# Halved weight sums and a two-step S4 in the paired projections of a fused two-block kernel

## The chip, the cores and the metric

The kernel runs on 1 core of one Trainium2 chip. The metric is the device time of one execution in microseconds (us). Five engines work side by side, each through its own queue in order: TensorE (PE, with its weight loads shown as PEld), VectorE (DVE), ScalarE (ACT), GpSimd (POOL) and SyncE (SP), which here only issues transfers.

## The reference, cut to what matters

Two transformer blocks follow each other on 1024 tokens of width 1024, in float32. The change touches two of the projections in them:

```
# pool layer of block 1
u, z = split(h @ w_in, [1024])              # w_in: 1024 x 2048
p    = multiscale_pool(u)                   # windowed means minus u
y    = ((einsum(p, w_mix) * scale) * silu(z)) @ w_out
# feed-forward of block 2
h    = h + square(relu(m @ w_up)) @ w_down  # w_up: 1024 x 4096
```

In both cases it is the first product (`h @ w_in` and `m @ w_up`) that is concerned.

## The kernel before, in words

Each float32 operand is written as a high and a low part (hi + lo), and each product takes three matmuls, hi by hi, lo by hi and hi by lo (`mm3`, L104, lines L108, L110 and L111). The high part is a copy on ScalarE, the low part the operand less the high part; `split_evac` (L117) does both, with the subtraction on VectorE unless another engine is named.

`project_pairs` (L327) computes a projection with a Winograd-type scheme of seven half-size products instead of eight. The activations, transposed, lie as quadrants A11, A12, A22 and the sums S1 to S4; the weights of a pair of column blocks (128 columns each, raw tiles r1 and r2) are turned into sums by `weight_sums` (L358, four subtractions on VectorE): the top half of r2, both halves of a third tile tt, and the bottom half of r1. `split_group` (L272) then splits such a raw tile of 128 x 1024 into `whi` (cast on ScalarE, L275) and `wlo` (subtraction on GpSimd, L276).

It is called twice: for the pool layer (L992, 8 pairs, NF=5) and for the feed-forward (L1952, 16 pairs, NF=4). Each call has two stretches.

- **The opening.** NF pairs do their first two products (`first_two`, A11 and A12), while the loop over j = 0 to 3 (L417) transposes the second half of the rows on TensorE (`turned`, L282), and `sums(j)` (L385) makes S2, A21 (for S1), A22, S3 and S4 of slice j, each with its hi and lo part. S4 = A12 - S2 is the last of them (L407), followed by its split (L408). A12 itself comes from the argument `a12`. In the feed-forward it lies there as a full float32 tile. In the pool layer it doesn't: GpSimd adds the high and the low part into a stage tile (L413), and L407 reads that. Between j = 1 and j = 2 the first pair's weights are summed (L435), and after j = 2 its tt tile is split (L437, `g0`).
- **The pairs.** `pair(p, ...)` (L443) sums and splits the weights and does S2, S1, S3, S4 and A22, of which S2 and S3 read the top half (LO) of a split tile and S1 and S4 the bottom half (HI). tt is split at L452, r2 at L457 and the bottom half of r1 at L467. All matmuls of one product go to one PSUM bank; there are 8 banks, and the bank of S2 and S3 is read by VectorE (`res.add`) before A22 may write it.

In the pool layer `Pooled` (L864) does the windowed sums of the finished u blocks on VectorE between the pairs (`doubled`, `less_u`, `cut`), with two tiny GpSimd products each (L949, L950), and zeroes the head of each u tile on GpSimd (L881). `stage()` (L846) there hands out eight half tiles in turn, cut from two u tiles, a z tile and a sum tile; the same pools hold the u and z blocks of the pairs.

The queues of the engines don't stand in the order of the source: a scheduler sets them when the program is built, by when it expects each instruction's inputs, and `issue_after` holds single instructions behind others. Buffers whi, wlo and wraw have three tiles each.

## Time and profile before

| what | value |
|---|---|
| median of 3 runs | 2354.05 us (2352.31 to 2356.96) |
| the profiled execution | 2356.74 us |
| its span, first to last instruction | 2354.9 us |
| mean granted TensorE clock | 0.990 of full |
| busy: PE / DVE / ACT / POOL | 2281.8 / 1504.1 / 1020.2 / 785.5 us |

The profile is of one execution. An engine's busy share is its time in instructions against the span. The pool layer's projection runs from about 450 to 640 us in the span, that of the feed-forward from about 1720 to 2025 us. A timeline row gives start, duration, engine, line, operation, output and inputs, and in square brackets the idle time before it with what ended it. A name is that of the first tile of a group, so the stage tiles appear as u, z and sum, and the line of a helper stands for all that call it.

### The profile page before, as it was taken

Reading aid. Unit: us, or ns where it says so; the run is one execution under the profiler, and the core shown is the slowest. Engines: PE = TensorE matmul, PEld = TensorE weight load, DVE = VectorE, ACT = ScalarE, POOL = GpSimd, SP = SyncE. Lnnn points to the kernel's source line nnn. Section 1 sums busy time; section 2 is a strip of 40 time slices with the busy share of each in tenths; the row PEclk is TensorE's granted clock in tenths of the full one; section 3 lists DMA queues with packets and bytes.
Section 4 is the critical chain, followed back from the end, with each engine's and each line's share of the span. In section 5 each row is a group of like instructions: output and inputs, shape, how many; then the busy total and the mean of one; then the engine's idle time right before and its main releaser. Section 6 shows DMA issues by size and latency. Waiting matters only on the chain.

```text
span 2354.9 us, 32237 instructions
## 1 busy us (share of the span) xinstructions
PE 2281.8 (97%) x11910; PEld 1900.3 (81%) x11910; DVE 1504.1 (64%) x2724; ACT 1020.2 (43%) x1921; POOL 785.5 (33%) x535
## 2 busy tenths in 40 slices
PE   7999999989998999999999999999999999999997
PEld 6877777867877888878988888888778888878886
DVE  5566676688788355554165746668785444687775
ACT  5344452543355354553232322423575555533334
POOL 2112123345532344431222112114324444454455
PEclk9999999999999999999999999999999999999999
DMA  4111013433372222211111111358145444754231
GB/s 159 39 28 37 19 36 108 134 85 108 111 256 94 63 59 68 54 59 46 46 47 52 50 54 44 122 181 312 65 136 197 149 150 171 279 209 171 101 125 72
DMA packets 248942, 253.10 MB, mean 107 GB/s; under 512 B 61064, under 2 KB 183006, under 8 KB 244944
## 3 DMA queue, kind: packets, MB, share of 16 engines
q1 hardware_dynamic: 239968, 233.38, 30.5%
q10 hardware_dynamic: 8224, 16.00, 1.8%
q0 software_dynamic: 592, 1.65, 0.3%
q8 instruction: 94, 1.54, 0.3%
q14 instruction: 64, 0.52, 0.1%
HBM read 181.26 MB, written 69.46 MB: 106 GB/s over the span
## 4 chain that ended last, share of the span: by engine, by line
PE 60%; DVE 11%; issue 3%; DMA 2%; ACT 2%; POOL 1%; SPq 0%; DVEq 0%; ACTq 0%; POOLq 0%
PE mm L110 18%; PE mm L108 18%; PE mm L111 18%; PE A L1550 2%; PE PT L1314 1%; DVE xl L119 1%; PE S L1291 1%; DVE sum L226 1%; PE tp L1570 1%; DVE raw L226 1%; DVE s L1303 1%; DVE xh L119 0%; DMA st<-d_y 0%; ACT ea L1050 0%; PE mm L282 0%
## 5 line engine op out<-in xcount | busy, mean ns | idle before, releaser
L108 PE MATMUL mm<-xh,whi 128*128 128x512 f32 (+2 forms) x1616 | 624.6, 387 | 11.6 <-DVE z L226 4.7
L110 PE MATMUL mm<-xl,whi 128*128 128x512 f32 (+2 forms) x1616 | 617.7, 382 | 0.0
L111 PE MATMUL mm<-xh,wlo 128*128 128x512 f32 (+2 forms) x1616 | 614.3, 380 | 0.2 <-POOL wlo L80 0.2
L80 POOL TENSOR_TENSOR wlo<-wraw,whi 128x1024 fp32r<-128x1024 f32 (+1 forms) x99 | 233.7, 2364 | 738.1 <-ACT whi L79 673.7
L108 PEld LDWEIGHTS mm<-xh,whi 128*128 128x128 f32 x1616 | 307.4, 190 | 70.1 <-DVE z L226 5.6
L111 PEld LDWEIGHTS mm<-xh,wlo 128*128 128x128 f32 x1616 | 307.1, 190 | 58.5 <-POOL wlo L80 0.5
L110 PEld LDWEIGHTS mm<-xl,whi 128*128 128x128 f32 x1616 | 307.5, 190 | 50.8
L111 PE MATMUL mm<-whi,xl 128*128 128x512 f32 (+1 forms) x752 | 272.0, 362 | 0.0
L79 ACT CAST whi<-wraw 128x1024 fp32r<-128x1024 f32 (+1 forms) x99 | 101.1, 1022 | 258.1 <-PE mm L110 146.0
L110 PE MATMUL mm<-wlo,xh 128*128 128x512 f32 (+1 forms) x560 | 197.1, 352 | 2.7 <-POOL wlo L80 1.4
L108 PE MATMUL mm<-whi,xh 128*128 128x512 f32 (+1 forms) x560 | 197.0, 353 | 1.8 <-DVE x L527 1.0
L110 PE MATMUL mm<-wlo,xl 128*128 128x512 f32 x416 | 163.3, 393 | 7.3 <-POOL wlo L119 4.3
L108 PE MATMUL mm<-whi,xl 128*128 128x512 f32 x416 | 163.1, 392 | 4.0 <-ACT whi L118 3.2
L276 POOL TENSOR_TENSOR wlo<-raw,whi 128x1024 fp32r<-128x1024 f32 (+1 forms) x59 | 122.8, 2084 | 114.5 <-ACT whi L275 111.9
L111 PEld LDWEIGHTS mm<-whi,xl 128*128 128x128 f32 x752 | 142.5, 189 | 21.7
L110 PEld LDWEIGHTS mm<-wlo,xh 128*128 128x128 f32 x560 | 105.9, 189 | 17.8 <-POOL wlo L80 2.0
L108 PEld LDWEIGHTS mm<-whi,xh 128*128 128x128 f32 x560 | 106.0, 189 | 16.4 <-DVE x L527 1.4
L276 POOL TENSOR_TENSOR wlo<-wraw,whi 128x1024 fp32r<-128x1024 f32 (+1 forms) x28 | 71.9, 2568 | 121.8 <-ACT whi L275 87.5
L119 POOL TENSOR_TENSOR wlo<-wraw,whi 128x1024 fp32r<-128x1024 f32 x28 | 73.7, 2636 | 108.9 <-ACT whi L118 86.9
L110 PEld LDWEIGHTS mm<-wlo,xl 128*128 128x128 f32 x416 | 78.5, 189 | 25.2 <-POOL wlo L119 5.5
L2019 DVE TENSOR_TENSOR X<-X,mm 128x512 f32<-128x512 f32 x112 | 73.1, 681 | 37.6 <-PE mm L111 37.6
L108 PEld LDWEIGHTS mm<-whi,xl 128*128 128x128 f32 x416 | 78.4, 189 | 22.5 <-ACT whi L118 4.4
(439 smaller groups left out, 4576.0 us busy)
## 6 DMA issues: line engine op xcount, KB each, us to landing
wraw<-in_w_in_dram SPq DMA_DIRECT2D x48, 512.0 KB, 3.7
d_S<-st SPq DMA_DIRECT2D x64, 256.0 KB, 4.6
raw<-in_w_up_dram SPq DMA_DIRECT2D x30, 512.0 KB, 5.7
d_A<-st ACTq DMA_DIRECT2D x48, 256.0 KB, 2.0
fa<-d_S SPq DMA_DIRECT2D x10, 1024.0 KB, 4.7
fa<-d_A SPq DMA_DIRECT2D x9, 1024.0 KB, 4.7
wraw<-in_attn_w_in_dram SPq DMA_DIRECT2D x32, 256.0 KB, 2.9
xh<-in_w_down_dram SPq DMA_DIRECT2D x16, 512.0 KB, 5.9
```

The costliest lines, as they stand in the source:

```text
L79: nc.scalar.copy(out=hv[:, i:i + n], in_=view[:, i:i + n])
L80: nc.gpsimd.tensor_tensor(out=lv[:, i:i + n], in0=view[:, i:i + n], in1=f(hv[:, i:i + n]), op=ALU.subtract)
L108: nc.tensor.matmul(ps, lhsT=lh[0], rhs=rh[0], start=first and i == 0, stop=False, skip_group_check=chain)
L110: nc.tensor.matmul(ps, lhsT=lh[0], rhs=rh[1], start=False, stop=False, skip_group_check=chain)
L111: nc.tensor.matmul(ps, lhsT=lh[1], rhs=rh[0], start=False, stop=last and i == n - 1, skip_group_check=chain)
L119: return (lo_eng or nc.vector).tensor_tensor(out=lo, in0=src, in1=f(hi), op=ALU.subtract)
L226: return nc.vector.tensor_tensor(out=out_, in0=x_, in1=y_, op=op)
L276: nc.gpsimd.tensor_tensor(out=lv, in0=view, in1=f(hv), op=ALU.subtract)
L1291: nc.tensor.matmul(sps[j], lhsT=(ql if n == 2 else qh)[rows, qsl], rhs=(kl if n == 1 else kh)[rows, ksl], start=n == 0, stop=n == 2)
L1303: nc.vector.tensor_scalar_mul(s, s, rs)
L1550: nc.tensor.matmul(aps[:, ch, :], lhsT=kc[:, ch * P:(ch + 1) * P], rhs=pat(Q, ch * P, n, nbc), start=True, stop=True)
L2019: added[:] = [nc.vector.tensor_tensor(out=dst, in0=dst, in1=banks[t], op=ALU.add)]
```

## The change

`split_group` gets two arguments: in how many equal pieces it cuts the tile, and which engine subtracts. Each piece is a `split_evac`. The tt tile of the first pair is split in two with the subtraction on VectorE; tt of the other pairs and r2 of all pairs are split in two with the subtraction on GpSimd, as before; r1 as a whole and its bottom half stay uncut. In the pool layer the addition of A12's parts on GpSimd goes, its stage tile with it, and S4 becomes two steps on VectorE: the high part less S2, then plus the low part. In the feed-forward S4 stays one step.

```
-    def split_group(view, n):
+    def split_group(view, n, cut=1, eng=nc.gpsimd):
         hv, lv = ...
-        nc.scalar.copy(out=hv, in_=view)
-        nc.gpsimd.tensor_tensor(out=lv, in0=view, in1=f(hv), op=ALU.subtract)
+        for i in range(0, n, n // cut):
+            sl = slice(i, i + n // cut)
+            split_evac(hv[:, sl], lv[:, sl], view[:, sl], eng)
         return hv, lv
...
-                vec(s2, a_, s2, ALU.subtract)
+                if there:
+                    vec(s2, a_, s2, ALU.subtract)
+                else:
+                    vec(s2, f(hl[0]), s2, ALU.subtract)
+                    vec(s2, s2, f(hl[1]), ALU.add)
                 split_evac(sh[4][0][:, j, :], sh[4][1][:, j, :], s2)
-            h, l = xx.at(4 + j, H0)
+            hl = xx.at(4 + j, H0)
             a_, there = a12(j)
-            if not there:
-                nc.gpsimd.tensor_tensor(out=a_, in0=f(h), in1=f(l), op=ALU.add)
             return rest
...
-                g0 = split_group(r0[2], KT)
+                g0 = split_group(r0[2], KT, 2, nc.vector)
...
-            g = split_group(tt, KT) if p else g0
+            g = split_group(tt, KT, 2) if p else g0
...
-            g = split_group(r2, KT)
+            g = split_group(r2, KT, 2)
...
-                      lambda j: (stage(), False), stage, raw_tile, opened, pooled, wu0, scaled[0], 5)
+                      lambda j: (None, False), stage, raw_tile, opened, pooled, wu0, scaled[0], 5)
```

## Rows read from the trace of the kernel before

**Rows 1.** The page's line of busy time for TensorE: busy us, share of the span, instructions.
```profile
PE 2281.8 (97%) x11910; PEld 1900.3 (81%) x11910; DVE 1504.1 (64%) x2724; ACT 1020.2 (43%) x1921; POOL 785.5 (33%) x535
```
**Rows 2.** The waits of TensorE from 440 to 660 us (the pool layer's projection): what waited, for what; us in total, times, longest.
```profile
PE mm L108 <- DVE z L226: 4.7, 2, 3.7
PE mm L111 <- POOL u L881: 2.5, 1, 2.5
PE mm L282 <- DVE z L226: 2.3, 1, 2.3
```
**Rows 3.** The waits of TensorE from 1690 to 2030 us (the feed-forward's projection), the longest of five.
```profile
PE mm L282 <- DVE st L1868: 2.2, 1, 2.2
```
**Rows 4.** Busy time and granted clock in stretches around 476 to 538 us. Columns: stretch, its length, busy time and count of PE, PEld, DVE, ACT, POOL, granted clock (1.00 is 2.4 GHz, 0.50 is 1.2 GHz), DMA share, GB/s.
```profile
479.00:486.00 7.00, 6.73 (x18) 5.13 (x19) 6.80 (x11) 4.93 (x9) 1.75 (x2) 0.52 1.02 277
494.00:498.00 4.00, 1.50 (x7) 0.91 (x6) 4.00 (x6) 1.78 (x3) 4.00 (x3) 1.00 0.00 0
498.00:504.00 6.00, 6.00 (x28) 4.88 (x27) 5.40 (x7) 3.35 (x6) 1.91 (x1) 1.00 0.01 3
...
532.00:538.00 6.00, 6.00 (x17) 4.68 (x17) 5.93 (x6) 3.69 (x5) 3.31 (x3) 0.59 0.00 0
```
**Rows 5.** Timeline of TensorE in the pool layer's opening and first two pairs.
```profile
478.95 1.12 PE L282 MATMUL mm<-ident,raw 128*128 128x128 f32 x4 [2.31 <-DVE z L226]
...
494.26 0.40 PE L110 MATMUL mm<-s2l,whi 128*128 128x512 f32 x1
497.15 0.50 PE L111 MATMUL mm<-s2h,wlo 128*128 128x512 f32 x1 [2.50 <-POOL u L881]
...
498.86 0.39 PE L108 MATMUL mm<-xh,whi 128*128 128x512 f32 x1
...
504.43 0.39 PE L108 MATMUL mm<-s2h,whi 128*128 128x512 f32 x1
...
507.85 0.39 PE L108 MATMUL mm<-s3h,whi 128*128 128x512 f32 x1
...
530.77 0.80 PE L108 MATMUL mm<-xh,whi 128*128 128x512 f32 x1 [3.72 <-DVE z L226]
```
**Rows 6.** Timeline of VectorE in the same stretch. The row at 475.21 is S4 of j = 0, that at 493.60 S4 of j = 2; 489.27 is the second of the four weight sums, which makes the top half of tt.
```profile
475.21 0.68 DVE L226 TENSOR_TENSOR u<-u 128x512 f32<-128x512 f32 x1
...
478.22 0.68 DVE L226 TENSOR_TENSOR z<-z,mm 128x512 f32<-128x512 f32 x1
...
489.27 0.68 DVE L226 TENSOR_TENSOR wraw<-wraw 128x512 f32<-128x512 f32 x1
...
493.60 0.69 DVE L226 TENSOR_TENSOR u<-u 128x512 f32<-128x512 f32 x1
...
494.80 0.75 DVE L392 SCALAR_TENSOR_TENSOR xl<-mm,vecs,xh 128x512 fp32r<-128x512 f32 x1
495.46 0.68 DVE L226 TENSOR_TENSOR ea<-ea,mm 128x512 f32<-128x512 f32 x1
496.06 1.59 DVE L119 TENSOR_TENSOR s4l<-u,s4h 128x512 fp32r<-128x512 f32 x1
...
502.99 0.69 DVE L119 TENSOR_TENSOR s2l<-sum,s2h 128x512 fp32r<-128x512 f32 x1 [0.60 <-ACT s2h L118]
...
526.13 2.85 DVE L226 TENSOR_TENSOR raw<-raw,wraw 128x512 f32<-128x512 f32 x1
...
530.04 0.67 DVE L226 TENSOR_TENSOR z<-z,mm 128x512 f32<-128x512 f32 x1
```
**Rows 7.** Timeline of GpSimd in the same stretch. 476.03 is the addition of A12's parts for j = 2, 493.06 the low part of the first pair's tt, 497.11 that of its r2, 525.07 that of the third pair's tt.
```profile
476.03 3.40 POOL L413 TENSOR_TENSOR u<-xh,xl 128x512 f32<-128x512 f32 x1 [13.81 <-DVE u L226]
...
493.06 4.04 POOL L276 TENSOR_TENSOR wlo<-wraw,whi 128x1024 fp32r<-128x1024 f32 x1 [6.78 <-ACT whi L275]
497.04 0.11 POOL L881 MEMSET u<- 128x16 f32 x1
497.11 2.80 POOL L276 TENSOR_TENSOR wlo<-wraw,whi 128x1024 fp32r<-128x1024 f32 x1
...
525.07 3.35 POOL L276 TENSOR_TENSOR wlo<-wraw,whi 128x1024 fp32r<-128x1024 f32 x1
```
**Rows 8.** Timeline of ScalarE in the same stretch: a whole cast of `split_group` and one of half the size.
```profile
491.93 1.05 ACT L275 CAST whi<-wraw 128x1024 fp32r<-128x1024 f32 x1
...
504.39 0.62 ACT L275 CAST whi<-wraw 128x512 fp32r<-128x512 f32 x1 [0.33 <-PE mm L110]
```
**Rows 9.** Groups of GpSimd instructions from 466 to 700 us, shapes apart: count, busy us, mean ns of one, idle before them.
```profile
L276 POOL TENSOR_TENSOR wlo<-raw,whi 128x1024 fp32r<-128x1024 f32 x10 | 26.9, 2694 | 15.0 <-ACT whi L275 12.4 <-DMA d_mS<-z 2.6
L276 POOL TENSOR_TENSOR wlo<-raw,whi 128x512 fp32r<-128x512 f32 x7 | 10.8, 1543 | 4.7 <-ACT whi L275 4.7
```
**Rows 10.** Busy time in the feed-forward's pairs, columns as in rows 4.
```profile
1800.00:2020.00 220.00, 220.00 (x964) 180.83 (x963) 96.68 (x128) 119.00 (x174) 98.25 (x47) 1.00 0.46 157
```
**Rows 11.** Timeline of TensorE in the feed-forward's opening.
```profile
1742.27 0.50 PE L108 MATMUL mm<-xh,whi 128*128 128x512 f32 x1 [0.32 <-DVE st L1868]
...
1747.95 0.39 PE L111 MATMUL mm<-s2h,wlo 128*128 128x512 f32 x1
```
**Rows 12.** Timeline of VectorE there.
```profile
1739.88 0.69 DVE L119 TENSOR_TENSOR s4l<-st,s4h 128x512 fp32r<-128x512 f32 x1 [0.90 <-ACT s4h L118]
1741.53 0.69 DVE L1868 TENSOR_TENSOR st<-st,mm 128x512 f32<-128x512 f32 x1 [0.95 <-PE mm L111]
```

## The prediction

> **What bounds the kernel now.** I read the busy line first, then the waits of TensorE in the two stretches that the change touches, then the timelines around the longest of these waits. The busy line says that TensorE works 97% of the span [rows 1]: a change that takes no matmul away can only win idle time of TensorE, some 73 us in the whole span, or time at the low clock. In the pool layer's projection three kinds of wait make 9.5 us [rows 2]; in that of the feed-forward the longest is 2.2 us [rows 3], and its pairs run without any gap, 220.00 us busy of 220 with VectorE, ScalarE and GpSimd each about half free [rows 10]. So whatever is split there in pairs 1 to 15 has nothing to win. What is left is the pool layer's opening and, less, the opening of the feed-forward.
>
> Three waits matter in the pool layer [rows 5]. **Wait 1**, 2.31 us before 478.95: the transposes need a bank that VectorE's addition at 478.22 frees [rows 6]. **Wait 2**, 2.50 us before 497.15: the first S2 product has its two matmuls with the high weights done, and the third needs the low weights. The row names a memset as releaser, but that is the next instruction on GpSimd's queue; what ended at 497.10 is the subtraction that began at 493.06 and took 4.04 us [rows 7]. **Wait 3**, 3.72 us before 530.77, again for an addition on VectorE, at 530.04. Waits 1 and 3 are followed by a stretch at 1.2 GHz (0.52 and 0.59 over stretches that are partly at 2.4 GHz), wait 2 is not [rows 4]. Such a stretch has a price: 17 matmuls in 6 us where the full clock does 28, so 11/28 of 6 us, 2.4 us.
>
> **The change part by part.**
>
> *S4 in two steps, pool layer only.* Four additions on GpSimd go (3.40 us for that of j = 2 [rows 7]); TensorE waited for none of them, so the gain is 0. VectorE gets four subtractions or additions of 128x512 more, at 0.60 us from start to start (495.46 to 496.06 [rows 6]). That of j = 0 follows the row at 475.21 and so stands ahead of the addition at 478.22 that ends wait 1: **+0.60 us on the path** (0 if the queue is ordered otherwise). That of j = 1 is hidden by TensorE's work from 479 to 494, in which it waits for nothing long; uncovered it would cost 0.60. That of j = 2 is counted with the next part. That of j = 3 lies behind 502.99, and S4 is multiplied only after S3, which starts at 507.85 [rows 5]: 0.
>
> *Stage tiles.* Three instead of four are taken for each j, so both u tiles are in use until j = 3 has its S3 and S4. The memset at 497.04 [rows 7] writes such a tile and now has to wait for j = 3, until about 504. Behind it on GpSimd stands the low part of the first pair's r2. Its first half would be there by 504 + 1.6 = 505.6, and S3 wants it at 507.85 or 1 us earlier: 0, with 1 us to spare; between 0 and about +1 us if the halves are slowed.
>
> *The first pair's tt (wait 2).* One cast of 1.05 us becomes two of 0.62 [rows 8], and 4.04 us on GpSimd become two subtractions of about 0.68 on VectorE. The top half needs only the second weight sum, at 489.27 to 489.95, so its cast can end near 490.6; if VectorE took it at once, TensorE would find it ready at 494.26: -2.50, the best end. But VectorE is full here. The latest place that its queue suggests is the one in which the addition at 495.46 stands, work that comes later in the source. Pushed by the second step of S4 of j = 2 (0.60) and by wait 1 (0.60), the half would end at 496.66 + 0.68 = 497.34 and TensorE go on at 497.4, against 497.15: +0.25 with the 0.60 of the first part in it. The best end with the same 0.60 is -1.9. Even an early half doesn't bring all of it: the fourth S2 product, at 504.43, waits for j = 3's low part, which starts at 502.99 on VectorE, and VectorE has 0.60 + 0.60 + 1.20 more to do before it, less 0.9 (the row at 496.06 takes 1.59 instead of 0.68 since GpSimd's 4.04 us are in its way), less the 0.60 it now waits for ScalarE: some 0.9 us later, with TensorE up to 1.9 earlier. S1 products can fill part of that. Between -1.9 and +0.25 I take **-1.0 for the opening, wait 1 included**, a little on the good side of the middle, because the top half is ready so early.
>
> *The other pairs' tt and all r2, halves on GpSimd.* 46 splits each get one cast more (2 x 0.62 - 1.05 = 0.19 us) and on GpSimd 2 x 1.54 - 2.69 = 0.4 us [rows 8, 9], 9 and 18 us in all. In the feed-forward they lie beside half-free engines [rows 10]. In the pool layer no wait of TensorE names a low part after the first pair [rows 2]: 0 directly. Indirectly it matters when VectorE is held up. Its row at 526.13 takes 2.85 us and ends at 528.98, 0.56 after GpSimd's subtraction of 525.07 to 528.42; a like row takes 0.68. The addition at 530.04 that ends wait 3 stands behind it. Two halves hold VectorE up as long as a whole if they come one after the other with a row of VectorE between, +0.3 by their longer sum; if VectorE gets its rows in ahead of the second half, some 1.1 us less. Between -1.1 and +0.4 I take **0**: the work on GpSimd that lies ahead of wait 3 is the same.
>
> The Trainium skill (SBUF — State Buffer, "Who interferes with whom") says that a VectorE instruction with two SBUF inputs and a GpSimd instruction that reads SBUF shut each other out for the whole length of the one that is first. The rows at 526.13 and 496.06 agree. By this rule alone, halves shorten each lock and not their sum.
>
> *Feed-forward opening.* The first pair's two subtractions go to VectorE here too, 2 x 0.60. VectorE idles 0.90 us before 1739.88 and 0.95 before 1741.53 [rows 12], where one fits; the second can delay the addition at 1741.53, for which TensorE already waits 0.32 [rows 11]. The low part itself isn't multiplied until 1747.95: nothing to win. Between 0 and +1.2, **+0.3**.
>
> Sum: -1.0 + 0 + 0.3 = -0.7 us. Against the profiled execution's own 2356.74 this is 2356.0. That execution stands 2.7 above the median of the runs shown, so I put the same difference on the median: 2354.05 - 0.7 = **2353.4**. About 0.2%, 4.7 us, is what a measurement of this kernel can tell from no change.
>
> **The rivals.**
>
> *VectorE loses less to GpSimd's halves (faster).* Wait 3 shrinks and the clock stays up after it. For: wait 2 of 2.50 us cost no low clock. Against: wait 1 of 2.31 us did [rows 4, 5]. Price: -0.7 for my sum, -1.1 for the lock, -0.9 for the opening at its best end, -0.7 at the second, 1.0 us wait for such an addition [rows 2], -2.4 for the clock: -5.8, 2348.3.
>
> *VectorE becomes the bound in the openings (slower).* The place is the same queue: the top half of the first tt is set behind the addition at 495.46 and S4's low part at 496.06. Then TensorE goes on at 497.4 + 0.60 + 0.60 = 498.6, 1.45 later than now. Its idle time is then about 3.5 us, near that of wait 3 [rows 5], and the clock falls: +2.4. In the feed-forward both halves come ahead of 1741.53: +1.2. Together +5.1, 2359.1. It decides if the half starts later than about 497.3, behind S4's low part of j = 2. For: VectorE has nearly no idle time here and gets six rows more. Against: the half is ready 4 us before TensorE asks.
>
> *The change doesn't do what it says.* The matmuls could wait for both halves, or the half stand so that TensorE goes on at 497.15 as before; then wait 1 is longer by 0.60, and there is no more to see: 2354.7.
>
> **How the numbers follow.** My forecast 0.58, with a range of its own of 2351.4 to 2355.7 (bounds -1.9, -1.1 and 0 below, rounded in for what partly excludes each other; +0.25, +0.4, +1.0 and +1.2 above, likewise); the change without effect 0.16; faster by VectorE's lesser loss 0.14; slower by VectorE 0.12. The likeliest case and the one without effect hold 0.74; the range reaches some way to the other two, to 2348.5 and 2358.0, and leaves out about half of each. Faster by over 0.2% (below 2349.3) is most of the third case with a little of the first: 0.16. Slower (above 2358.8) is most of the fourth: 0.11. The rest, 0.73, is within 0.2%.
>
> **What would show it.** In the profile after: wait 1 near 2.9 us with its stretch at 1.2 GHz; wait 2 at or under 1.5 us, ended by VectorE (the low half, or a row that frees a bank), no wlo of the first pair's tt on GpSimd, and the fourth S2 product within 1 us of where it stood against wait 1's end; wait 3 between 2.6 and 4.2 us; the feed-forward's pairs still without a gap. I am wrong if wait 3 and the low clock behind it are gone, if a new stretch at 1.2 GHz stands near 498, or if TensorE loses time in places that the diff doesn't touch.

## The result and the profile after

The changed kernel took 2361.32 us in the median of 7 runs (2358.64 to 2362.03), the kernel before 2354.05 beside it: ratio 1.0028, interval 1.0018 to 1.0037. A second measurement, in the experiments below, gave 1.0016 (1.0007 to 1.0024). The change is slower by 4.6 to 6.5 us, 0.2 to 0.3 per cent. My 2353.4 with the range 2348.5 to 2358.0 was wrong.

The busy line of the kernel after, against [rows 1], shows no engine with much more to do; TensorE is busy 1.6 us longer, in a span that is 4.8 us longer:

```profile
PE 2283.4 (97%) x11910; PEld 1899.1 (80%) x11910; DVE 1503.4 (64%) x2732; ACT 1025.8 (43%) x1969; POOL 786.9 (33%) x575
```

The waits of TensorE in the kernel after, 440 to 660 us (what waited, for what; us in total, times, longest), to be read beside [rows 2]:

```profile
PE mm L108 <- DVE z L226: 5.0, 2, 3.7
PE mm L283 <- DVE z L226: 2.7, 1, 2.7
PE mm L110 <- DVE u L119: 2.0, 1, 2.0
PE mm L108 <- DVE ea L226: 1.5, 1, 1.5
PE mm L108 <- DVE xl L393: 1.3, 1, 1.3
...
```

The 2.5 us for GpSimd's low part is gone, and two waits for VectorE, 1.3 and 1.5 us, stand in its place. Where they lie is in the timeline of TensorE, the kernel after; its four longest waits of the opening answer to [rows 5]:

```profile
479.33 1.11 PE L283 MATMUL mm<-ident,raw 128*128 128x128 f32 x4 [2.68 <-DVE z L226]
...
487.38 0.47 PE L108 MATMUL mm<-xh,whi 128*128 128x512 f32 x1 [1.34 <-DVE xl L393]
...
500.98 0.50 PE L108 MATMUL mm<-xh,whi 128*128 128x512 f32 x1 [1.52 <-DVE ea L226]
...
505.25 0.39 PE L108 MATMUL mm<-s2h,whi 128*128 128x512 f32 x1
...
531.52 0.80 PE L108 MATMUL mm<-xh,whi 128*128 128x512 f32 x1 [3.67 <-DVE z L226]
```

TensorE has its products of the opening later than before although the wait that was to go did go: wait 3 ends 0.75 us later. VectorE's timeline in the kernel after shows what stands in the way; it answers to [rows 6]. The rows `u<-xh,u` and `u<-u,xl` are the two steps of S4 (476.18 is the second step of j = 0), and `wlo` at 496.24 and 498.55 are the first pair's halves:

```profile
476.18 0.69 DVE L226 TENSOR_TENSOR u<-u,xl 128x512 f32<-128x512 f32 x1
...
478.59 0.69 DVE L226 TENSOR_TENSOR z<-z,mm 128x512 f32<-128x512 f32 x1
...
482.81 0.69 DVE L226 TENSOR_TENSOR wraw<-wraw 128x512 f32<-128x512 f32 x1 [1.02 <-DMA wraw<-in_pool_w_in_dram]
483.42 0.68 DVE L119 TENSOR_TENSOR s2l<-z,s2h 128x512 fp32r<-128x512 f32 x1
...
495.64 0.68 DVE L226 TENSOR_TENSOR u<-xh,u 128x512 f32<-128x512 f32 x1
496.24 0.69 DVE L119 TENSOR_TENSOR wlo<-wraw,whi 128x512 fp32r<-128x512 f32 x1
496.85 1.78 DVE L226 TENSOR_TENSOR u<-u,xl 128x512 f32<-128x512 f32 x1
498.55 1.77 DVE L119 TENSOR_TENSOR wlo<-wraw,whi 128x512 fp32r<-128x512 f32 x1
500.25 0.68 DVE L226 TENSOR_TENSOR ea<-ea,mm 128x512 f32<-128x512 f32 x1
500.84 0.68 DVE L119 TENSOR_TENSOR s4l<-u,s4h 128x512 fp32r<-128x512 f32 x1
```

From 495.64 on they follow each other without a gap, and the row at 500.25 that TensorE waits for stands behind them; S4's second step and the second half take 1.8 us each beside GpSimd's halves of r2. And there is a row that none of my steps spoke of: at 482.81 stands the first of the four weight sums of the first pair, ahead of the low part of S2 of j = 1, and VectorE waits 1.02 us for its load. In the kernel before it stood at 487.60, behind j = 1's S4. GpSimd in the same kernel:

```profile
496.58 3.19 POOL L119 TENSOR_TENSOR wlo<-wraw,whi 128x512 fp32r<-128x512 f32 x2 [45.06 <-ACT whi L118]
```

The clock around waits 1 to 3, kernel after, columns as in [rows 4], is the same as before to the digit (0.52, 1.00 and 0.59), so the loss between these two traces isn't one of the clock there:

```profile
479.00:486.00 7.00, 6.41 (x16) 4.51 (x16) 5.98 (x11) 3.67 (x7) 0.00 (x0) 0.52 0.96 270
...
498.00:504.00 6.00, 4.48 (x20) 3.33 (x19) 6.00 (x8) 2.83 (x5) 1.77 (x2) 1.00 0.00 0
532.00:538.00 6.00, 6.00 (x17) 4.66 (x17) 5.93 (x7) 3.71 (x7) 2.97 (x3) 0.59 0.00 1
...
1800.00:2020.00 220.00, 220.00 (x964) 180.81 (x963) 94.47 (x129) 120.26 (x198) 102.24 (x71) 1.00 0.46 156
```

Its last row is that of the feed-forward's pairs, to be read beside [rows 10]: no gap, the same 964 matmuls. The pairs cost nothing. Their opening does. Timeline of TensorE, the kernel after, in the feed-forward:

```profile
1752.39 0.39 PE L111 MATMUL mm<-xh,wlo 128*128 128x512 f32 x1
1753.10 0.50 PE L108 MATMUL mm<-s2h,whi 128*128 128x512 f32 x1 [0.32 <-ACT s2h L118]
1753.87 0.50 PE L108 MATMUL mm<-xh,whi 128*128 128x512 f32 x1 [0.27 <-ACT xh L118]
...
1756.41 0.40 PE L111 MATMUL mm<-s3h,wlo 128*128 128x512 f32 x1
```

These waits have no counterpart before; in [rows 11] the products of that place start from 1747.95 on without waiting. The waits are only part of the loss: from 1752.39 to 1756.41 TensorE starts nine matmuls in 4.02 us, and at the 0.23 us from start to start that the rows just before show (1751.71, 1751.94, 1752.17, 1752.39) it would have needed 2.07. So 2.0 us are lost here. VectorE there, the kernel after, beside [rows 12]:

```profile
1743.14 0.74 DVE L393 SCALAR_TENSOR_TENSOR st<-mm,vecs,fa 128x512 f32<-128x512 f32 x1
1743.80 1.09 DVE L119 TENSOR_TENSOR wlo<-wraw,whi 128x512 fp32r<-128x512 f32 x1
1744.81 1.39 DVE L393 SCALAR_TENSOR_TENSOR st<-mm,vecs,st 128x512 f32<-128x512 f32 x2
1746.13 0.67 DVE L119 TENSOR_TENSOR wlo<-wraw,whi 128x512 fp32r<-128x512 f32 x1
...
1750.39 0.74 DVE L393 SCALAR_TENSOR_TENSOR st<-mm,vecs,fa 128x512 f32<-128x512 f32 x1
```

VectorE in the kernel before, the first weight sum of the pool layer and the place in the feed-forward that answers to 1743.14 and 1750.39:

```profile
487.60 0.69 DVE L226 TENSOR_TENSOR wraw<-wraw 128x512 f32<-128x512 f32 x1
...
1742.13 1.41 DVE L392 SCALAR_TENSOR_TENSOR st<-mm,vecs,fa 128x512 f32<-128x512 f32 x2
1743.45 2.12 DVE L392 SCALAR_TENSOR_TENSOR st<-mm,vecs,st 128x512 f32<-128x512 f32 x3
```

At 1742.13 two rows `st<-mm,vecs,fa` followed each other, the S3 of slice j = 2 and that of j = 3. Now the second comes at 1750.39, behind the two halves and behind the rest of j = 2, and with it everything that j = 3 is made of. In the old order there was room for two more rows: the S2 of j = 3 is one of the three at 1743.45, ended by 1745.57, and TensorE in the kernel before takes it up 4.0 us later:

```profile
1749.56 0.39 PE L108 MATMUL mm<-s2h,whi 128*128 128x512 f32 x1
```

In the table are three lengths, each between starts that the views by line give: **pool** from the first transposition of z on TensorE (L282 before, at 450.5) to ScalarE's last copy at L919 (657.4); **slices** from VectorE's S4 low part (`s4l`) of j = 0 to that of j = 3 (477.0 to 507.2); **feed-forward** from the first transposition of Xb (1720.5) to ScalarE's last copy at L1864 (2024.4). Lines are those of the kernel before.

| kernel | pool | slices | feed-forward |
|---|---|---|---|
| before, first trace | 206.9 | 30.2 | 303.9 |
| after | 206.6 | 32.7 | 305.0 |

In this pair of traces the pool stage isn't longer after, though wait 3 ends later in it, and the feed-forward is longer by 1.1 us where the count above has 2.0. Each length also holds stretches at 1.2 GHz, and these differ between executions; the experiments come back to it.

### The profile page after: what moved, and what is told of

It reads as the page before. It is cut to its first block, busy times and chain, and to the rows that moved or that the text cites. A ratio compares the mean times of both kernels' runs of the same rounds, so it can differ in the third digit from the quotient of the medians.

```text
span 2359.7 us, 32327 instructions
## 1 busy us (share of the span) xinstructions
PE 2283.4 (97%) x11910; PEld 1899.1 (80%) x11910; DVE 1503.4 (64%) x2732; ACT 1025.8 (43%) x1969; POOL 786.9 (33%) x575
## 4 chain that ended last, share of the span: by engine, by line
PE 75%; DVE 13%; issue 5%; DMA 3%; ACT 2%; POOL 1%; SPq 0%; ACTq 0%; DVEq 0%; POOLq 0%
PE mm L110 22%; PE mm L108 22%; PE mm L111 21%; PE A L1553 2%; PE PT L690 1%; PE S L672 1%; PE PT L1317 1%; DVE xl L119 1%; PE S L1294 1%; DVE sum L226 1%; PE tp L1573 1%; DVE raw L226 1%; DVE wlo L119 1%; DVE r L132 1%; DMA xh<-in_w_down_dram 1%
## 5 line engine op out<-in xcount | busy, mean ns | idle before, releaser
L80 POOL TENSOR_TENSOR wlo<-wraw,whi 128x1024 fp32r<-128x1024 f32 (+1 forms) x99 | 234.1, 2368 | 737.5 <-ACT whi L79 663.4
L119 POOL TENSOR_TENSOR wlo<-wraw,whi 128x512 fp32r<-128x512 f32 (+1 forms) x78 | 146.7, 1894 | 259.4 <-ACT whi L118 237.4
L119 POOL TENSOR_TENSOR wlo<-raw,whi 128x512 fp32r<-128x512 f32 (+1 forms) x81 | 128.8, 1602 | 117.0 <-ACT whi L118 115.2
L118 ACT CAST whi<-wraw 128x512 fp32r<-128x512 f32 (+1 forms) x104 | 77.2, 768 | 120.9 <-PE mm L111 39.9
L110 PEld LDWEIGHTS mm<-wlo,xl 128*128 128x128 f32 x416 | 78.7, 189 | 25.5 <-POOL wlo L119 5.5
L108 PEld LDWEIGHTS mm<-whi,xl 128*128 128x128 f32 x416 | 78.9, 190 | 24.7 <-ACT whi L118 5.0
```

Source lines behind the costliest of these rows:

```text
L80: nc.gpsimd.tensor_tensor(out=lv[:, i:i + n], in0=view[:, i:i + n], in1=f(hv[:, i:i + n]), op=ALU.subtract)
L108: nc.tensor.matmul(ps, lhsT=lh[0], rhs=rh[0], start=first and i == 0, stop=False, skip_group_check=chain)
L110: nc.tensor.matmul(ps, lhsT=lh[0], rhs=rh[1], start=False, stop=False, skip_group_check=chain)
L118: nc.scalar.copy(out=hi, in_=src)
L119: return (lo_eng or nc.vector).tensor_tensor(out=lo, in0=src, in1=f(hi), op=ALU.subtract)
```

## The experiments

Every kernel was timed in 11 runs beside the kernel before on the same chip. Ratios are to the kernel before, with 95% intervals; a difference is that of the means, with twice its standard error.

**The same program, the change again, and its two parts.** `same_again` is the kernel before; `change_pool_only` has all edits of the pool layer's projection and none of the feed-forward's (the new arguments are given where NF is 5), `change_feed_forward_only` the other way round.

```
-  g = split_group(r2, KT, 2)
+  g = split_group(r2, KT, 2 if NF > 4 else 1)     # the same for tt and g0; NF == 4 in the other kernel
```

> The kernel before, unchanged. Both theories: ratio 1.000, within 0.1%. What it is for is the trace: whether the granted clock after the three waits near 1645 to 1655 us stays at 1.00 as in the first trace of before, or falls by itself from run to run (the luck theory says it may fall here too, 1.6 us; the cause theory says it stays), and how far two traces of one program lie apart at the start of the down projection (near 2053 us).

> The whole change again, its lines kept where they stand in the kernel before. Ratio 1.003 (1.002 to 1.004). Cause theory: the trace loses at the same places as the first trace of after: about 1.6 us of low clock behind 1655, 1.2 us in the feed-forward's opening, 1.9 us before the first addition of the down projection, near 0 in the pool layer. Luck theory: the low clock behind 1655 or the 1.9 us is gone in this trace and the time of single runs varies by it.

> The change in the pool layer's projection alone (S4 in two steps, all halves there, the first pair's on VectorE); the feed-forward's projection as before. Theory 1, the loss is made in the feed-forward: 2354 us, ratio 0.9995 to 1.001, the feed-forward's opening and the start of the down projection as in before. Theory 2, the pool layer's part moves the rest of the program and the clock falls later: 2355.5 to 2358, ratio 1.0006 to 1.0015, with a low clock behind 1655.

> The change in the feed-forward's projection alone (all halves there, the first pair's on VectorE); the pool layer as before. Theory 1: 2357 to 2358, ratio 1.0012 to 1.0018, with 1.2 us lost in the feed-forward's opening and 1.9 us before the first addition of the down projection. Theory 2: 2354 to 2355, ratio below 1.0008.

| kernel | median us | ratio | difference us |
|---|---|---|---|
| same program | 2354.20 | 0.9999 (0.9990 to 1.0008) | -0.3 ± 1.2 |
| change again | 2359.23 | 1.0016 (1.0007 to 1.0024) | +4.6 ± 1.2 |
| pool layer only | 2356.04 | 1.0006 (0.9998 to 1.0015) | +1.4 ± 0.9 |
| feed-forward only | 2356.64 | 1.0010 (1.0001 to 1.0018) | +2.9 ± 2.0 |

The parts add up, 1.4 + 2.9 against 4.6. The change again lost less than the 1.002 to 1.004 expected. Both parts lose, the feed-forward more, where I had expected least; the pool layer's loss is near the edge of what these runs can tell (its ratio's interval holds 1).

The traces of single executions must be read with care. In the first trace of the kernel after, 1.7 us of its loss came near 1655, where the diff touches nothing. The granted clock of 1650 to 1662 us is 0.86 there. The row of that stretch (columns as in [rows 4]) in the kernel before:

```profile
1650.00:1662.00 12.00, 8.56 (x36) 6.51 (x36) 12.00 (x12) 5.05 (x5) 0.27 (x1) 1.00 0.00 0
```

and in `same_again`, which is the kernel before once more:

```profile
1650.00:1662.00 12.00, 9.01 (x32) 7.13 (x33) 12.00 (x14) 6.14 (x8) 1.61 (x1) 0.86 0.00 0
```

The same program has the stretch at 1.2 GHz in one execution and not in another. So that loss is chance and no part of the change.

The same chance sits in the lengths of the feed-forward. In the eleven traces of this document's kernels whose feed-forward is as before, it takes 302.9 to 303.1 us in six and 303.9 to 304.1 in five, the first trace of before among these. In the six the stretch at 1.2 GHz behind the wait near 1731 lacks 1.7 us of full clock (worked out as in the last section), in the five 3.4. The three traces with the change's whole feed-forward part take 304.9 to 305.0, all with 1.7: like with like they lose 2.0 us and not 1.1, which is what the count of TensorE's starts gave.

**Taking the feed-forward's part apart.** `feed_forward_first_pair` has only the first pair's two halves on VectorE, `feed_forward_halves` only the other halves, on GpSimd; `feed_forward_all_on_gpsimd` has all halves, those of the first pair on GpSimd too.

```
-  g0 = split_group(r0[2], KT, 2, nc.vector)
+  g0 = split_group(r0[2], KT, 2, nc.gpsimd)       # feed_forward_all_on_gpsimd
```

> Only the feed-forward is changed, and there only the first pair's weight sum: two halves, subtracted on VectorE; all other splits whole, on GpSimd. Theory 1 (the feed-forward part costs 1.0 us in its opening, because VectorE has no room there, and up to 2 us more at the handover to the down projection, because the halves on GpSimd set one load one place later in SyncE's queue): 1720 to 2024 us takes 304.9 instead of 303.9, the handover 28.9, and the time is the kernel before plus 1.0, about 2355.5. Rival A (the 1.0 us is made by the halves on GpSimd): 303.9 and no difference, 2354.5. Rival B (the handover is slow in some runs whenever the pairs end later): 304.9, with the handover at 30.9 in some runs, plus 2 to 3 us.

> Only the feed-forward is changed, and there only tt of pairs 1 to 15 and r2 of all pairs: two halves each on GpSimd; the first pair's tt whole, on GpSimd. Theory 1: 1720 to 2024 us takes 303.9 as before, the handover 28.9 in some runs and 30.9 in others, so the runs lie in two groups some 2 us apart and the mean is plus 0.5 to plus 2, 2355 to 2356.5. Rival A (the halves on GpSimd make the opening 1.0 us longer): 304.9, plus 1 at least. Rival C (halves cost nothing and the slow handover has another cause): 303.9, 28.9, 2354.5.

> Only the feed-forward: all halves of the change, but those of the first pair's tt subtracted on GpSimd instead of VectorE. Theory 3 (the feed-forward's loss is the two subtractions on VectorE in its opening: the first stands in line behind a lock by GpSimd, and the S3 row of slice j = 3 comes 6 us later than before): VectorE's rows stand as before, no wait of TensorE on s2h and xh near 1751, 1720 to 2024 us takes 303.9 to 304.2, and the time is plus 0 to 0.7 against the kernel before, 2354.6 to 2355.3. Rival F (the loss is made by halving itself, or by the other order of TensorE's products, wherever the subtraction stands): 304.9 or more, plus 1 to 4.

| kernel | median us | ratio | difference us | feed-forward us |
|---|---|---|---|---|
| first pair on VectorE | 2358.54 | 1.0019 (1.0010 to 1.0028) | +4.4 ± 1.3 | 307.5 |
| other halves, GpSimd | 2355.03 | 1.0002 (0.9993 to 1.0011) | +0.5 ± 1.3 | 304.5 |
| all halves on GpSimd | 2355.55 | 1.0008 (0.9999 to 1.0017) | +1.0 ± 1.2 | 304.4 |

The first pair's two rows on VectorE alone cost no less than the whole part (the 1.5 us between the two are inside their errors). Expected were 304.9 and +1.0; the place was right and the size four times too small. For the other halves 303.9 was expected; their 304.5, and the 304.4 of the last row, stand beside 303.9 to 304.1, since both traces have the 3.4 us of missing clock. VectorE in `feed_forward_first_pair`:

```profile
1739.92 0.74 DVE L392 SCALAR_TENSOR_TENSOR st<-mm,vecs,fa 128x512 f32<-128x512 f32 x1
1740.59 2.63 DVE L119 TENSOR_TENSOR wlo<-wraw,whi 128x512 fp32r<-128x512 f32 x1
1743.14 1.40 DVE L392 SCALAR_TENSOR_TENSOR st<-mm,vecs,st 128x512 f32<-128x512 f32 x2
...
1748.73 0.74 DVE L392 SCALAR_TENSOR_TENSOR st<-mm,vecs,fa 128x512 f32<-128x512 f32 x1
```

GpSimd in the same kernel:

```profile
1740.26 2.41 POOL L119 TENSOR_TENSOR wlo<-wraw,whi 128x1024 fp32r<-128x1024 f32 x1 [39.63 <-ACT whi L118]
```

and TensorE:

```profile
1749.18 0.39 PE L111 MATMUL mm<-xh,wlo 128*128 128x512 f32 x1
1751.43 0.49 PE L108 MATMUL mm<-s2h,whi 128*128 128x512 f32 x1 [1.86 <-ACT s2h L118]
1752.20 0.70 PE L108 MATMUL mm<-xh,whi 128*128 128x512 f32 x1 [0.28 <-ACT xh L118]
...
1755.94 0.40 PE L108 MATMUL mm<-s3h,whi 128*128 128x512 f32 x1
```

VectorE's half starts 0.33 us after GpSimd's whole subtraction and ends 0.55 after it: 2.63 us for a row of 0.68. The rule of the Trainium skill that the prediction weighed (SBUF — State Buffer, "Who interferes with whom") agrees with this row. S3 of j = 3 comes 8.8 us behind that of j = 2 (1748.73 and 1739.92), where it followed within 0.7 us before. TensorE runs dry for 1.86 us, and its matmuls from 1752.20 to 1755.23 take 0.6 to 0.8 us each; the granted clock of 1750 to 1758 is 0.79. From 1749.18 to 1755.94 it starts ten matmuls in 6.76 us, where 2.3 were enough: 4.5 us lost in this one place, which is the whole +4.4 of the runs, and the 307.5 against 303.0. In the whole change GpSimd's halves are shorter and the same row takes 1.09; there the place costs 2.0 us, and the clock doesn't fall behind it. That the halves make this difference fits the rows, but the runs (+2.9 ± 2.0 and +4.4 ± 1.3) don't tell the two apart.

With all halves on GpSimd, the S3 rows of j = 2 and j = 3 stand together again on VectorE, as in the kernel before:

```profile
1740.89 1.40 DVE L392 SCALAR_TENSOR_TENSOR st<-mm,vecs,fa 128x512 f32<-128x512 f32 x2
```

TensorE waits for no s2h and xh there, and most of the loss is gone. Rival F, that halving itself or another order of TensorE's products makes the loss, isn't borne out by the stage (304.4, and it asked for 304.9 or more), but the time, +1.0, lies at the lower end of its +1 to +4 and above the 0.7 of theory 3. TensorE's order of products differs from before in this kernel too, though it isn't that of the change. What is left, +0.5 and +1.0, lies inside the intervals.

Theory 1 had a second half: that the handover to the down projection (2024 to 2053 us) is slower in some executions because one load stands a place later in SyncE's queue. It took 30.8 us in the kernel after and 31.0 in `change_feed_forward_only`, where SyncE waited 2.5 us for a load of `fa`, against 28.9 before; but 29.1 in `change_again`, 29.0 with the first pair alone and 28.5 with the halves, which have the later load. Neither half of the change brings it out alone. What makes it stays open.

**Taking the pool layer's part apart.** Two kernels without the halves first, then two without S4's second step.

```
-  vec(s2, f(hl[0]), s2, ALU.subtract)
-  vec(s2, s2, f(hl[1]), ALU.add)
+  vec(s2, a_, s2, ALU.subtract)                   # pool_halves, pool_first_pair_and_halves:
                                                   # A12's parts added on GpSimd, as before
```

> Only the pool layer's S4 is made in two steps on VectorE from A12's high and low part; all splits are whole, on GpSimd. Theory 2 (the pool part moves VectorE's work about and is worth nothing): wait 1 at 2.3 to 2.9 us, the wait for the first pair's low part 2.5 us or less, 450 to 657 us takes 206.9 plus 0 to 0.6, and the time 2354.5 to 2355.2. Rival D (the two more rows for each slice on VectorE are what the pool part's 1.5 us are): plus 1.5, 2356.

> Pool layer only: S4 in two steps and the first pair's tt in two halves on VectorE; tt of the other pairs and r2 whole on GpSimd, and the feed-forward as before. Theory 2: the wait for the first pair's low part is gone, a wait of 1.3 to 2 us on a bank stands in its place, the second stage starts 0 to 0.8 us later, 450 to 657 us takes 206.5 to 206.9, and the time is 2354.2 to 2354.6. Rival D (these rows on VectorE are the pool part's cost of 1.5 us): 2356. Rival E (the halves on GpSimd are that cost): 2353.5 to 2354.5, at least 1 us under the pool part as a whole.

> Pool layer only: tt of pairs 1 to 7 and r2 of all pairs in two halves on GpSimd; S4 and the first pair's tt as before. Theory 4 (in the pool layer the two-step S4 costs, 2 us, and the halves give back 1): wait 3 stays at 3.7 us and VectorE's rows beside GpSimd's get shorter, 450 to 657 us less its low clock is about 1 us shorter, and the time is 2353.5 to 2354. Rival G (the halves do nothing in the pool layer): 2354.6.

> Pool layer only, the change without its two-step S4: the first pair's tt in halves on VectorE, the other halves on GpSimd, A12's parts added on GpSimd as before. Theory 4 (the cost of the pool part is S4's second row): under the pool part as a whole by 1 to 2 us, 2353.5 to 2354.6, and wait 1 back at 2.3 us. Rival H (the first pair's halves on VectorE cost as in the feed-forward): 2356 or more.

And the dose: the kernel before with one row more on VectorE for each slice, and nothing else.

```
   vec(s2, a_, s2, ALU.subtract)
+  if not there: vec(s2, s2, s2, ALU.max)
```

> The kernel before with one redundant row on VectorE for each slice of the pool layer's opening (S4 written over itself, as the greater of itself and itself, 128x512): four rows of 0.60 us, all else as before, A12's parts still added on GpSimd. Theory 4 (VectorE sets the pace of the pool layer's opening, so each row on it is paid): plus 1.5 to 2.4 us, 2356.1 to 2357. Rival G (the pool part's loss isn't in VectorE's rows): plus 0 to 0.6, 2354.6 to 2355.2.

| kernel | median us | ratio | difference us | pool us | slices us |
|---|---|---|---|---|---|
| S4 in two steps | 2357.03 | 1.0008 (0.9999 to 1.0017) | +1.7 ± 1.5 | 206.9 | 32.8 |
| S4 and first pair | 2356.99 | 1.0008 (0.9999 to 1.0016) | +2.3 ± 1.3 | 209.2 | 34.6 |
| pool part as a whole | 2356.04 | 1.0006 (0.9998 to 1.0015) | +1.4 ± 0.9 | 206.7 | 32.0 |
| halves | 2355.22 | 1.0006 (0.9997 to 1.0015) | +0.6 ± 1.1 | 205.1 | 28.9 |
| first pair and halves | 2353.63 | 1.0001 (0.9992 to 1.0009) | -0.9 ± 1.1 | 205.3 | 28.8 |
| one more row per slice | 2355.91 | 1.0007 (0.9999 to 1.0016) | +1.5 ± 1.2 | 207.5 | 33.1 |

The runs speak for rival D and for theory 4: by their medians the two kernels with S4 and without halves lose more than theory 2 allows (the interval of the first, from +0.2 on, still touches it), and without S4's second step the pool part loses nothing. Rival E, that the halves are the cost, falls with the second row of the table. The column of the slices sorts them. In six traces with the pool layer as before it is 29.4 to 31.1 (mean 30.3), in six with the two-step S4 32.0 to 34.6 (33.2), with the dose 33.1, and in six with halves or first pair but a one-step S4 28.8 to 29.3. A row on VectorE seems to be paid, whether it computes something or not: four rows at 0.60 are 2.4 us, the dose costs 2.8 between the slices. The waits of TensorE with the dose, 440 to 660 us, look like those after, with a longer wait 1 and a wait for `xl`:

```profile
PE mm L282 <- DVE z L226: 2.9, 1, 2.9
PE mm L108 <- DVE xl L392: 2.5, 1, 2.5
```

Only the first of the two is a sign of the added rows: the kernels with S4 in one step and halves have wait 1 at 2.3 us and yet wait 1.0 to 2.2 us for `xl`. I took theory 4 for settled all the same: VectorE sets the pace, each row on it is paid. Rival H falls in any case: the first pair's halves on VectorE, dear in the feed-forward, cost nothing in the pool layer. What the halves alone do there, -1.3 us by the length of the stage (205.1 against a mean of 206.4 in the six traces as before) and +0.6 ± 1.1 by the runs, isn't settled.

**The change without its costs.** `whole_but_feed_forward_pair_on_gpsimd` is the change with the feed-forward's first pair on GpSimd; `change_without_its_two_costs` has the one-step S4 besides; two kernels were timed again.

```
-  g0 = split_group(r0[2], KT, 2, nc.vector)
+  g0 = split_group(r0[2], KT, 2, nc.vector if NF > 4 else nc.gpsimd)
```

> The whole change, but the halves of the feed-forward's first tt subtracted on GpSimd instead of VectorE. Theory 3: only the pool layer's part is left, plus 1.5 with 0.5 for the feed-forward's halves at most: 2356 to 2356.6, 3 us under the whole change. Rival F: 2358.5 to 2360 as the whole change.

> The whole change without S4's second step (A12's parts are added on GpSimd as before) and with the halves of the feed-forward's first tt on GpSimd; the pool layer's first tt in halves on VectorE and all other halves on GpSimd stay. Theories 3 and 4 together: minus 0.9 for the pool layer's rest and plus 0 to 1.0 for the feed-forward's halves, so 2353.7 to 2355.6, 4 to 5 us under the whole change. If a third cause is at work: 2356.5 or more.

> The same kernel as the pool layer's first pair and halves without S4's second step. If it is faster than the kernel before, its mean is again 0.9 us lower, 2353.7; if that was chance, 2354.2 to 2355.

> The same kernel a third time. If it is faster than the kernel before: mean 1 to 2.5 us lower, 2352 to 2353.5. If not: 2354.2 to 2355.

> The same kernel a second time: 2352.5 to 2354 if the feed-forward's halves on GpSimd cost nothing beside the pool layer's gain, 2354.5 to 2355.5 if they cost the 1 us that two single runs hinted at.

| kernel | median us | ratio | difference us |
|---|---|---|---|
| change, feed-forward's pair on GpSimd | 2357.09 | 1.0015 (1.0006 to 1.0024) | +2.7 ± 1.3 |
| the same, S4 in one step | 2352.65 | 0.9996 (0.9987 to 1.0004) | -1.2 ± 1.3 |
| the same again | 2354.71 | 1.0001 (0.9992 to 1.0010) | +0.3 ± 1.4 |
| pool layer's first pair and halves, again | 2352.01 | 0.9988 (0.9979 to 0.9997) | -2.7 ± 0.9 |
| the same, third time | 2353.47 | 0.9995 (0.9986 to 1.0004) | -0.6 ± 1.1 |

Each of the two costs, taken out, gives back its share: 1.8 ± 1.8 us (4.6 to 2.7) for the feed-forward's pair, where 3 were expected, and 3.2 ± 1.6 more (2.7 to a mean of -0.5) for S4. No third cause is needed (S4's share is looked into below). The pool layer's first pair and halves alone are the best version run: -0.9, -2.7 and -0.6, a mean of -1.4 ± 0.6 us. That beats the change clearly and the kernel before by less than a single measurement can tell; one of its three intervals leaves 1 out.

**The same rows in another order.** The dose had a flaw that a view of VectorE's idle time in all traces showed. In each of the seven with a row more per slice, the dose among them, VectorE waits 0.8 to 1.4 us for a weight load near 482, as at 482.81 above; in none of the twelve others. The added rows had also moved the first pair's weight sums ahead of j = 1's work; without such rows the sums stand behind j = 1's S4, as at 487.60 above. The last kernel is the pool part as a whole, two-step S4 included, with these sums held behind the S4 of j = 1.

```
-  ready = {1: weight_sums(*r0)}
+  with tc.issue_after(s4_):            # s4_: the low part of S4 of j = 1
+      ready = {1: weight_sums(*r0)}
```

> The pool layer's part of the change as a whole, two-step S4 included, but the first pair's weight sums are held behind the split of S4 of j = 1, so that VectorE doesn't wait for their load ahead of j = 1's work. Theory 5 (of S4's cost of 2.8 us some 1 us is that the first weight sum was set too early and waits 1.0 us for a load): no wait of VectorE for a load near 482, the slices (first to last s4l) take 31.0 us instead of 32.0, and the time is plus 0.2 to 0.7, 2354.6 to 2355.2. Rival I (the rows alone are the cost, the wait only fills time that would be idle anyway): slices 32.0 or more, plus 1.4 as the pool part, 2355.8 to 2356.2. Rival J (the sums held back make the first tt late): slices 31.0, but TensorE waits for the first pair's whi or wlo, and the time is no better than plus 1.4.

It took 2353.91 us, ratio 0.9996 (0.9987 to 1.0005), a difference of -1.1 ± 1.2 against +1.4 ± 0.9 with the sums where the scheduler had set them. The stage takes 205.3 us, the slices 31.4. TensorE's waits, 440 to 660 us:

```profile
PE mm L108 <- DVE z L226: 4.6, 2, 3.3
...
PE mm L108 <- DVE xl L392: 0.5, 1, 0.5
```

The wait for `ea` is gone and that for `xl` is 0.5 us. VectorE in the same kernel:

```profile
485.66 0.68 DVE L226 TENSOR_TENSOR z<-z,xl 128x512 f32<-128x512 f32 x1
...
488.40 0.69 DVE L226 TENSOR_TENSOR ea<-ea,mm 128x512 f32<-128x512 f32 x1 [1.40 <-PE mm L111]
...
496.34 0.68 DVE L226 TENSOR_TENSOR u<-u,xl 128x512 f32<-128x512 f32 x1
496.94 0.68 DVE L119 TENSOR_TENSOR wlo<-wraw,whi 128x512 fp32r<-128x512 f32 x1
497.55 0.68 DVE L226 TENSOR_TENSOR ea<-ea,mm 128x512 f32<-128x512 f32 x1
```

S4's second step of j = 1 starts 1.5 us earlier than in the kernel after (485.66 against 487.15, with wait 1 over 0.4 earlier), VectorE now waits for TensorE at 488.40 instead of the other way round, and the bank's addition stands at 497.55 instead of 500.25. Of these 2.7 us, 2.2 come from two rows that took 1.78 and 1.77 beside GpSimd's halves of r2 and take 0.68 each here; the same two halves take GpSimd 5.94 us in this trace and 3.19 after.

Theory 5 holds, and better than expected: the order makes the loss, and more of it than the 1 us that the theory gave to the load. The rows do lengthen the slices, 31.4 us against the 28.8 to 29.3 with S4 in one step, about what four rows take; but this length is not the cost. TensorE's own place says more. From the first transposition of z to the end of wait 3 it takes 79.1 us here, as in the six traces with S4 in one step and halves (78.9 to 79.3); in the six with S4 in two steps it takes 80.7 to 82.9, with the dose 82.2, and in the six as before 78.4 to 82.3. By the runs -1.1 ± 1.2 here stands against -1.4 ± 0.6 without S4's rows: what is left of their cost is 0.3 ± 1.3 us, where four rows at 0.60 would have made 2.4. Theory 4, that each row is paid, falls with it; the dose had moved the same sums, and a dose with the sums held was not run. Rival I falls, and so does J, since no wait names the first pair's `whi` or `wlo`. Which of the changed places counts most, the load that is waited for, the later place of j = 1's chain or the meeting with GpSimd, this run doesn't separate: the hold changes several places in both queues.

## Why the prediction was wrong

- **What bounds the kernel: half right.** TensorE's waits were the place to look, and the feed-forward's pairs were costed at nothing and cost nothing: 220.00 us busy of 220 after as before. What I took from the trace of before beyond that was the order of VectorE's queue, and both failures come from there. That wait 2 cost no low clock was also a reading of one execution: in three of the six traces with the pool layer as before, `same_again` among them (granted clock 0.57 from 496 to 500), it did.
- **S4 in two steps, +0.60 within the -1.0 of the opening: this step failed, by the order that it took for fixed.** I set the added rows into the queue as it stood and asked what each delays. Wait 1 did go from 2.31 to 2.68, and the rows of j = 1 and j = 3 are in fact hidden, or nearly: with the order held the pool part with S4 is at -1.1, without S4 at -1.4, and I had -1.0. What I didn't ask is what the scheduler does with the rows around them. It set the weight sums ahead of j = 1, and the pool part cost +1.4 ± 0.9 instead of the -1.0. The sentence "0 if the queue is ordered otherwise" had one side only: the order could get better for a row, and not worse for others.
- **The first pair's tt and the halves, pool layer: right by the number, the split between them open.** Without S4's 0.60 I had -1.6; the runs gave -1.4 ± 0.6 (three measurements). I gave all of it to the first pair and none to GpSimd's halves. No run has the first pair's halves alone with S4 in one step, and the trace with GpSimd's halves alone reaches the end of wait 3 as early (79.0 us), while its time, +0.6 ± 1.1, shows no gain. In the kernel after, wait 2 for the low part went, two waits for VectorE's bank rows came (1.34 and 1.52, expected one of up to 1.5), and the fourth S2 product at 505.25 stands 25.9 us behind wait 1's end against 25.5.
- **Stage tiles, 0: right, for another reason.** The memset that could have held up r2's low part stands at 506.40 in the kernel after, behind the first pair's three subtractions on GpSimd, so nothing waited for it.
- **Feed-forward's opening, +0.3 between 0 and +1.2: this step failed, by size and for the same reason.** Alone it costs +4.4, within the whole change some +1.8 to +2.9 by the runs and 2.0 by TensorE's starts. I had looked for idle time into which two rows fit and found 0.90 and 0.95. The queue didn't put them there: the first stands behind 1743.14, and the scheduler set the S3 row of j = 3, which needed nothing but its turn, behind the rest of j = 2. The price was not the row's 0.6 us but the 6 to 8 us by which a neighbour lost its place. That the loss goes when VectorE's old order comes back was shown, with the two rows off VectorE as well; that the rows alone would have fitted rests on the 4.0 us of room in the trace of before. A run with the halves on VectorE and j = 3 held in its place was not made.
- **GpSimd's halves, 0: right within the error** (+0.5 and +1.0, each ± 1.3, in the feed-forward).
- **The base.** The median after, 2361.32, lies beside its profiled run, 2361.51; before it lay 2.7 under. Setting a sum against one execution carries that scatter, and so do traces set side by side.
- **The rivals.** The slower one had the right engine, both openings, and a time, 2359.1, that the second measurement met within 0.2. That is luck: 2.4 of its 5.1 us were for a clock that didn't fall. Its place was wrong: no low clock near 498 (1.00 in the row above), and the half stood early, at 496.24. Its condition, a half later than 497.3, was not met for the first half, and the loss came all the same, from rows set elsewhere. At 0.12 it had too little: a changed order was one more way to lose in each opening, and no rival held it. The wait 3 of the faster rival stayed at 3.67, its clock at 0.59. Of the signs of being wrong that I named, only the last came, time lost where the diff touches nothing: 1.7 us near 1655, which is chance, and 1.9 in the handover behind the feed-forward, which `change_again` doesn't have (29.1).

## What to carry to other kernels

Where a scheduler sets the queues, don't price an added row in the old order: ask which neighbours may change places, above all a row whose load lands late and a row that needs only its turn, and give that case a chance and a bound of its own. Two rows of 0.6 us cost 4.4 us here and four cost 2.8 ± 1.1 (+1.4 against -1.4 without them) by what they moved, and the four 0.3 ± 1.3 once the order was held. Before a dose is believed, compare its queues with those of the kernel that it doses: it may move what the change moves.

## What the runs showed of the hardware

- **The clock falls at different places in executions of one program.** In the kernel before it fell near 1456 and not at 1652 in one trace, and the other way round in the other. Worked out as the time in 4 us slices at their missing clock, a stretch lacks 1.7 or 3.4 us (2.4 in my sum), and an execution 17 to 24 us in all. Two traces of one program differ by 2 to 3.5 us in this (23.3 and 19.8 in the two of the kernel before), half of what was to be explained here. It is an estimate of what the clock costs at most, since TensorE would have waited through part of it.
- **A VectorE row beside GpSimd can take four times its length**: 2.63 us at 1740.59 against 0.68, and over 0.5 us of it after GpSimd's row had ended. Beside GpSimd's halves the same row takes 1.09. GpSimd can lose too: two halves that take 3.19 us together in the kernel after take 5.94 with the sums held back, while VectorE's rows beside them take 0.68; and its row of 4.04 us in [rows 7] ran beside VectorE's of 0.69 at 493.60 [rows 6].
- **A handover between two stages has two lengths**, 28.3 to 29.6 and 30.8 to 31.0 us, with a load's landing as the only difference seen; it was long in two of three traces that hold the whole feed-forward part, and its cause is open.
